# Average pooling over windows of 16: VectorE sums whole tiles, GpSimd's fold stays in the last two tiles

## The chip, the cores and the metric

The kernel runs on one core of one Trainium2 chip. The time is the device time of one execution in microseconds (us), as the median of several executions. A separate execution is recorded by the hardware profiler; its span runs from the first to the last instruction of the core.

## The reference

The input is 32 x 256 rows of 4096 float32 values, and the output has 256 values for each row. Each output is the mean of its own window of 4096 / 256 = 16 neighbouring values:

```python
for i in range(output_size):
    start = int(i * length / output_size)
    end = int((i + 1) * length / output_size)
    result[:, :, i] = np.mean(x[:, :, start:end], axis=-1)
```

134.2 MB are read and 8.4 MB are written. There is one addition for each value read, and nothing is read twice.

## The kernel before

The 8192 rows are cut into 16 tiles of 512 rows. In a tile each of the 128 partitions holds four rows, that is 1024 windows ("cells") of 16 values, 64 KB; a tile is 8.39 MB. Tiles 0 to 14 are laid out so that a partition's rows, and its outputs, are contiguous over the fifteen tiles (`x_many`, `o_many`); the last tile is laid out by itself.

There are two input buffers, `xin0` and `xin1`, used in turn, and one result tile `res` that holds the sums of all 16 tiles. SyncE issues all loads (line 63). The first two go out at once. Each later one, that of tile t + 2, is issued after SyncE has waited for the semaphore `summed` to say that tile t has been summed (line 100), because it overwrites the same buffer.

A tile is worked on as follows, with m = 512, half of the cells:

- GpSimd waits for the landing of the tile and folds the second half of the cells in place: in each window the last eight values are added to the first eight (line 81).
- VectorE waits for the same landing, sums the first half's windows of 16 (line 88), then waits for GpSimd's fold (semaphore `folded`, line 89) and sums the second half's windows, by now of eight (line 90). That instruction counts `summed` up.
- ScalarE waits for `summed` and multiplies the tile's 1024 sums by 1/16 in place (line 95), counting `scaled` up.

Each engine takes its instructions in the order in which they are written, and only the semaphores order the engines among each other. After the loop SyncE issues the store of tiles 0 to 14 when 15 tiles have been scaled (line 105), then that of the last tile (line 107). Both stand in the same DMA queue as the loads.

Of the kernel before, what the change touches and what calls it, by code (L numbers as in the profile page):

```python
# [1 line left out]

# [4 lines left out]


@with_exitstack
def kernel(  # L10
    ctx: ExitStack,
    tc: tile.TileContext,
    x: bass.AP,
    output_size: int,
    out: bass.AP,
):
    nc = tc.nc
    F32 = mybir.dt.float32
    X = mybir.AxisListType.X

    batch, channels, length = x.shape
    ob, oc, olen = out.shape
    assert ob == batch and oc == channels and olen == output_size
    assert length % output_size == 0
    window = length // output_size
    hw = window // 2
    inv_w = 1.0 / float(window)

    P = nc.NUM_PARTITIONS
    R = 4  # L30
    rows = batch * channels
    assert rows % (P * R) == 0
    ntiles = rows // (P * R)
    many = (ntiles - 1) * R
    cells = R * output_size
    m = cells // 2
    cols = R * length

    xr = x.rearrange("b c l -> (b c) l")
    orow = out.rearrange("b c o -> (b c) o")  # L40
    x_many = xr[0 : P * many, :].rearrange("(p r) l -> p (r l)", p=P, r=many)
    o_many = orow[0 : P * many, :].rearrange("(p r) o -> p (r o)", p=P, r=many)
    x_last = xr[P * many :, :].rearrange("(p r) l -> p (r l)", p=P, r=R)
    o_last = orow[P * many :, :].rearrange("(p r) o -> p (r o)", p=P, r=R)

    nbuf = 2
    xin = [
        nc.alloc_sbuf_tensor(f"xin{i}", [P, cells, window], F32, align_bytes=256)
        for i in range(nbuf)
    ]  # L50
    res = nc.alloc_sbuf_tensor("res", [P, ntiles * cells], F32, align_bytes=256)


    landed = [nc.alloc_semaphore(f"landed{i}") for i in range(nbuf)]
    folded = nc.alloc_semaphore("folded")
    summed = nc.alloc_semaphore("summed")
    scaled = nc.alloc_semaphore("scaled")
    stored = nc.alloc_semaphore("stored")

    def load(t):  # L60
        src = x_last if t == ntiles - 1 else x_many[:, t * cols : (t + 1) * cols]
        dst = xin[t % nbuf][:, :, :].rearrange("p o w -> p (o w)")
        dma = nc.sync.dma_start(out=dst, in_=src)  # L63
        dma.then_inc(landed[t % nbuf], 16)
        return dma.ins.name

    for t in range(nbuf):  # L70
        tc.info.no_tile_sem_insts.add(load(t))
    tc.close()
    tc.compile()  # L73

    for t in range(ntiles):
        xt = xin[t % nbuf]
        lo, mid, hi = t * cells, t * cells + m, (t + 1) * cells
        here = 16 * (t // nbuf + 1)

        nc.gpsimd.wait_ge(landed[t % nbuf], here)  # L80
        nc.gpsimd.tensor_add(  # L81
            out=xt[:, m:cells, 0:hw],
            in0=xt[:, m:cells, 0:hw],
            in1=xt[:, m:cells, hw:window],
        ).then_inc(folded, 1)

        nc.vector.wait_ge(landed[t % nbuf], here)
        nc.vector.reduce_sum(out=res[:, lo:mid], in_=xt[:, 0:m, :], axis=X)  # L88
        nc.vector.wait_ge(folded, t + 1)
        nc.vector.reduce_sum(  # L90
            out=res[:, mid:hi], in_=xt[:, m:cells, 0:hw], axis=X
        ).then_inc(summed, 1)

        nc.scalar.wait_ge(summed, t + 1)
        nc.scalar.mul(  # L95
            out=res[:, lo:hi], in_=res[:, lo:hi], mul=inv_w
        ).then_inc(scaled, 1)

        if t + nbuf < ntiles:
            nc.sync.wait_ge(summed, t + 1)  # L100
            load(t + nbuf)

    done = (ntiles - 1) * cells
    nc.sync.wait_ge(scaled, ntiles - 1)
    nc.sync.dma_start(out=o_many, in_=res[:, 0:done]).then_inc(stored, 16)
    nc.sync.wait_ge(scaled, ntiles)
    nc.sync.dma_start(out=o_last, in_=res[:, done:]).then_inc(stored, 16)
    for s in (*landed, folded, summed, scaled):
        nc.sync.sem_clear(s)
    nc.sync.wait_ge(stored, 32)  # L110
    nc.sync.sem_clear(stored)


# [1 line left out]
_INS = ['x', 'output_size']  # L115
_OUTS = [((32, 256, 256), 'float32')]

_NUMBERS = {'output_size': 256}


# [26 lines left out]
```

## Time and profile before

| | |
|---|---|
| median of 3 runs | 333.61 us (333.47 to 333.75) |
| the profiled execution | 333.56 us, span 332.3 us |
| bytes read, written | 134.22 MB, 8.39 MB |
| mean rate over the span | 429 GB/s |
| VectorE (DVE) busy | 209.7 us, 63% |
| GpSimd (POOL) busy | 139.7 us, 42% |
| ScalarE (ACT) busy | 18.2 us, 5% |

In the profile's rows DVE is VectorE, POOL is GpSimd, ACT is ScalarE and SPq is the sequencer of SyncE, which issues the DMAs. A group's row gives the line of the kernel, the engine, the operation, the tile written and the tiles read with their shapes (partitions x elements), the count, then busy time in all, the mean of one in ns, and the idle time of the engine ahead of them with what ended it. A row of the timeline gives the start, the duration, the instruction, and in brackets the engine's idle time ahead of it and what ended that. The landing of a load is the moment at which its semaphore has its full count.

### The profile page before, as it was taken

Reading aid. Unit: us, or ns where it says so; the run is one execution under the profiler, and the core shown is the slowest. Engines: PE = TensorE matmul, PEld = TensorE weight load, DVE = VectorE, ACT = ScalarE, POOL = GpSimd, SP = SyncE. Lnnn points to the kernel's source line nnn. Section 1 sums busy time; section 2 is a strip of 40 time slices with the busy share of each in tenths; the row PEclk is TensorE's granted clock in tenths of the full one; section 3 lists DMA queues with packets and bytes.
Section 4 is the critical chain, followed back from the end, with each engine's and each line's share of the span. In section 5 each row is a group of like instructions: output and inputs, shape, how many; then the busy total and the mean of one; then the engine's idle time right before and its main releaser. Section 6 shows DMA issues by size and latency. Waiting matters only on the chain.

```text
span 332.3 us, 130 instructions
## 1 busy us (share of the span) xinstructions
DVE 209.7 (63%) x32; ACT 18.2 (5%) x17; POOL 139.7 (42%) x20
## 2 busy tenths in 40 slices
DVE  0029396692939669292966939295693929568392
ACT  1000101001010100001010000101000010100001
POOL 0028091542709164270906437090633709063370
DMA  9898999989898999989898998989899998989997
GB/s 379 379 505 379 489 394 434 450 379 505 379 497 387 473 410 402 481 379 505 379 497 387 434 450 379 505 379 505 379 481 402 426 458 379 505 379 497 371 473 300
DMA packets 2592, 142.61 MB, mean 429 GB/s; under 512 B 288, under 2 KB 288, under 8 KB 416
## 3 DMA queue, kind: packets, MB, share of 16 engines
q1 hardware_dynamic: 2592, 142.61, 99.4%
HBM read 134.22 MB, written 8.39 MB: 429 GB/s over the span
## 4 chain that ended last, share of the span: by engine, by line
DMA 66%; POOL 21%; DVE 11%; ACT 0%; issue 0%; SPq 0%
DMA xin<-in_x_dram 66%; POOL xin L81 21%; DVE res L90 11%; ACT res L95 0%; SPq L63 0%
## 5 line engine op out<-in xcount | busy, mean ns | idle before, releaser
L81 POOL TENSOR_TENSOR xin<-xin 128x4096 f32<-128x4096 f32 x16 | 139.5, 8718 | 181.7 <-DMA xin<-in_x_dram 181.7
L88 DVE TENSOR_REDUCE res<-xin 128x512 f32<-128x8192 f32 x16 | 139.0, 8686 | 114.7 <-DMA xin<-in_x_dram 114.7
L90 DVE TENSOR_REDUCE res<-xin 128x512 f32<-128x4096 f32 x16 | 70.7, 4420 | 1.8
L95 ACT ACTIVATE res<-res 128x1024 f32<-128x1024 f32 x16 | 16.9, 1056 | 306.7 <-DVE res L90 306.7
L95 ACT ACT_TABLE_LOAD x1 | 1.3, 1283 | 2.4 <-PEq L73 2.4
L128 POOL MEMSET const-float32-0.0<- 128x1 f32 x1 | 0.1, 98 | 0.2 <-issue 0.2
L128 POOL MEMSET const-bfloat16-1.0<- 128x1 bf16 x1 | 0.1, 101 | 0.0
L128 POOL MEMSET const-uint8-127<- 128x1 uint8 x1 | 0.1, 101 | 0.0
L128 POOL MEMSET const-float32-1.0<- 128x1 f32 x1 | 0.1, 98 | 0.0
## 6 DMA issues: line engine op xcount, KB each, us to landing
out_dram<-res SPq DMA_DIRECT2D x1, 7680.0 KB, 23.4
out_dram<-res SPq DMA_DIRECT2D x1, 512.0 KB, 5.0
xin<-in_x_dram SPq DMA_DIRECT2D x16, 25.4
```

The source lines that it names most:

```text
L81: nc.gpsimd.tensor_add(out=xt[:, m:cells, 0:hw], in0=xt[:, m:cells, 0:hw], in1=xt[:, m:cells, hw:window],).then_inc(folded, 1)
L88: nc.vector.reduce_sum(out=res[:, lo:mid], in_=xt[:, 0:m, :], axis=X)
L90: nc.vector.reduce_sum(out=res[:, mid:hi], in_=xt[:, m:cells, 0:hw], axis=X).then_inc(summed, 1)
L95: nc.scalar.mul(out=res[:, lo:hi], in_=res[:, lo:hi], mul=inv_w).then_inc(scaled, 1)
L128: nc = _bacc.Bacc("TRN2", target_bir_lowering=False, num_devices=1)
```

## The change

For tiles 0 to 13 (`behind`, the number of tiles that are left, is over 2) VectorE sums all 1024 windows of 16 values in one instruction, which counts `summed` up; GpSimd has nothing to do. For tiles 14 and 15 the work stays as it was: GpSimd folds the second half, VectorE sums the first, waits for the fold, and sums the second. The count that VectorE waits for becomes 1 and 2 there. Loads, multiplies and stores are not edited.

```diff
+        behind = ntiles - t
 
         nc.vector.wait_ge(landed[t % nbuf], here)
-        nc.vector.reduce_sum(out=res[:, lo:mid], in_=xt[:, 0:m, :], axis=X)
-        nc.vector.wait_ge(folded, t + 1)
-        nc.vector.reduce_sum(
-            out=res[:, mid:hi], in_=xt[:, m:cells, 0:hw], axis=X
-        ).then_inc(summed, 1)
+        if behind <= 2:
+            nc.gpsimd.wait_ge(landed[t % nbuf], here)
+            nc.gpsimd.tensor_add(
+                out=xt[:, m:cells, 0:hw],
+                in0=xt[:, m:cells, 0:hw],
+                in1=xt[:, m:cells, hw:window],
+            ).then_inc(folded, 1)
+            nc.vector.reduce_sum(out=res[:, lo:mid], in_=xt[:, 0:m, :], axis=X)
+            nc.vector.wait_ge(folded, 3 - behind)
+            nc.vector.reduce_sum(
+                out=res[:, mid:hi], in_=xt[:, m:cells, 0:hw], axis=X
+            ).then_inc(summed, 1)
+        else:
+            nc.vector.reduce_sum(
+                out=res[:, lo:hi], in_=xt[:, :, :], axis=X
+            ).then_inc(summed, 1)
```

The fold and its wait, which stood ahead of VectorE's wait for every tile, are the lines under `if behind <= 2` now.

More of the change, by code (lines that the diff above doesn't have):

```diff
@@ L78 @@
         here = 16 * (t // nbuf + 1)
[L80 to L85, printed above, removed]
-        nc.vector.wait_ge(landed[t % nbuf], here)
-        nc.vector.reduce_sum(out=res[:, lo:mid], in_=xt[:, 0:m, :], axis=X)
-        nc.vector.wait_ge(folded, t + 1)
-        nc.vector.reduce_sum(
-            out=res[:, mid:hi], in_=xt[:, m:cells, 0:hw], axis=X
-        ).then_inc(summed, 1)
+        behind = ntiles - t
+        nc.vector.wait_ge(landed[t % nbuf], here)
+        if behind <= 2:
[14 more added lines that the diff above has]
+            ).then_inc(summed, 1)
         nc.scalar.wait_ge(summed, t + 1)
```

## The prediction

> **What bounds the kernel now.** I read the page first, then the groups by line, then the timeline around one tile, and last the DMA share in chosen stretches.
>
> ```profile
> span 332.3 us, 130 instructions
> ...
> q1 hardware_dynamic: 2592, 142.61, 99.4%
> ...
> DMA 66%; POOL 21%; DVE 11%; ACT 0%; issue 0%; SPq 0%
> ...
> L81 POOL TENSOR_TENSOR xin<-xin 128x4096 f32<-128x4096 f32 x16 | 139.5, 8718 | 181.7 <-DMA xin<-in_x_dram 181.7
> L88 DVE TENSOR_REDUCE res<-xin 128x512 f32<-128x8192 f32 x16 | 139.0, 8686 | 114.7 <-DMA xin<-in_x_dram 114.7
> L90 DVE TENSOR_REDUCE res<-xin 128x512 f32<-128x4096 f32 x16 | 70.7, 4420 | 1.8
> ```
>
> The chain that ended last gives POOL 21% and DVE 11%, as if a third of the time hung on arithmetic. The queue's line says otherwise: packets keep the 16 DMA engines busy for 99.4% of the span. Both are true, because the chain steps back through "the buffer came free" even where the freed buffer's load then stood in line behind another load. The timeline shows that line:
>
> ```profile
> 31.62 4.42 DVE L90 TENSOR_REDUCE res<-xin 128x512 f32<-128x4096 f32 x1
> 36.07 19.62 SPq L63 DMA_DIRECT2D xin<-in_x_dram  x2
> ...
> 42.11 8.69 DVE L88 TENSOR_REDUCE res<-xin 128x512 f32<-128x8192 f32 x1 [6.07 <-DMA xin<-in_x_dram]
> 42.16 8.72 POOL L81 TENSOR_TENSOR xin<-xin 128x4096 f32<-128x4096 f32 x1 [10.57 <-DMA xin<-in_x_dram]
> 50.91 4.42 DVE L90 TENSOR_REDUCE res<-xin 128x512 f32<-128x4096 f32 x1
> ...
> 61.44 8.69 DVE L88 TENSOR_REDUCE res<-xin 128x512 f32<-128x8192 f32 x1 [6.12 <-DMA xin<-in_x_dram]
> ```
>
> Tile 0 is started on at 22.82 us, tile 1 at 42.11, tile 2 at 61.44: one tile every 19.32 us. VectorE is done with tile 0 at 36.04, SyncE issues the load of tile 2 at 36.07 (0.03 later), and that load waits behind the load of tile 1 until about 41 to 42 us. So the kernel is bound by its transfers, and the compute has a **lead** of 6.07 us over them, VectorE's idle time ahead of each tile. What matters is whether a load still has a predecessor in the queue when it is issued, and that needs the time that a load takes into an empty queue. Only the first load shows it:
>
> ```profile
> L63 SPq DMA_DIRECT2D xin<-in_x_dram x16: 327/328/426, 0.7 to 287.2; - x16
> ...
> DMA to landing us min/median/max: 22.1/25.4/40.9
> ```
>
> The least time to landing, 22.1, is this one's: issued at 0.74, VectorE begins at 22.82, so 22.08 us. The DMA share by stretch takes it apart (columns: stretch, its length, busy time of DVE, ACT and POOL, clock, DMA share, GB/s; a packet counts whole in the stretch in which it starts, hence shares above 1):
>
> ```profile
> 0.00:1.75 1.75, 0.00 (x0) 0.00 (x0) 0.20 (x4) 1.00 0.00 0
> 1.75:2.12 0.37, 0.00 (x0) 0.00 (x0) 0.00 (x0) 1.00 8.04 2657
> 2.12:2.63 0.51, 0.00 (x0) 0.25 (x1) 0.00 (x0) 1.00 0.00 0
> 2.63:2.64 0.01, 0.00 (x0) 0.01 (x1) 0.00 (x0) 1.00 16.16 6554
> ...
> 12.00:20.00 8.00, 0.00 (x0) 0.00 (x0) 0.00 (x0) 1.00 1.19 516
> 21.70:22.47 0.77, 0.00 (x0) 0.00 (x0) 0.00 (x0) 1.00 3.15 1362
> 22.47:24.10 1.63, 1.28 (x1) 0.00 (x0) 1.23 (x1) 1.00 0.00 0
> 24.00:32.00 8.00, 7.89 (x2) 0.00 (x0) 7.59 (x1) 1.00 1.19 516
> ```
>
> No packet starts in the 1.0 us after the issue. Then 15 engines start a 64 KB packet each between 1.75 and 2.12 (2657 GB/s for 0.37 us is 15 x 65536 bytes), and the 16th at 2.63. The 15 take 8.04 x 0.37 x 16 / 15 = 3.17 us each, the late one 16.16 x 0.01 x 16 = 2.59. A packet with a predecessor takes 3.15 x 0.77 = 2.42 us. Each engine carries 8 of them in a load (8.39 MB over 16 engines, 64 KB each): 8 x 2.42 = 19.35, the 19.32 of the period. The second load's packets have all started by 22.47, so the first load ended there, and VectorE began 0.36 us later. An empty queue thus costs 22.08 - 19.34 = 2.74 us beyond the data: 1.0 to the first packet, up to 0.4 of spread (1.9 on the late engine), 0.75 for the slower first packet, 0.36 at the end.
>
> **The change, part by part.**
>
> *VectorE.* For tiles 0 to 13, 8.69 + 4.42 us in two instructions become one over 16384 elements, which no row shows. The two rows give the slope: (8686 - 4420) / 4096 = 1.0415 ns per element, and 4420 - 4096 x 1.0415 = 154 ns fixed. So 154 + 16384 x 1.0415 = **17.22 us**. The upper bound is twice the half tile, 17.37; the lower is 17.06, with no fixed part. I take the line through both rows. GpSimd ran beside the 8686 and not beside the 4420, and one slope with a small constant fits both, so I count nothing for GpSimd's absence. Against today's 31.62 + 4.42 - 22.82 = 13.22 us VectorE holds the tile 4.00 us longer, and the lead shrinks from 6.07 to 2.07 us. VectorE itself stays under the 19.32 of a tile and is no bound.
>
> *GpSimd.* Fourteen folds of 8.72 us and 14 waits of VectorE for them go. They lay beside VectorE's first half (8.72 against 8.69), so what they held up is inside the 13.22. That they no longer touch memory buys the transfers nothing: the share is 1.19 from 12 to 20 us, where no engine works, and 1.19 from 24 to 32, where VectorE and GpSimd both do.
>
> *ScalarE, SyncE.* The multiply (1.06 us) starts 4 us later and frees no buffer. SyncE's wait before each load moves from 13.22 to 17.22 us after the landing. Queued behind it on SyncE are only later loads and the stores, so nothing else is held. No store is moved past anything: the large one goes out after tile 14, which is still folded.
>
> *The loads.* This is the term that decides. Load t+2 goes out 17.22 + 0.03 = 17.25 us after tile t's start. If it finds the queue as the first load did, it lands 22.08 us later, less 0.10 because the first issue took 426 ns and the usual one 328: 21.98. So tile t+2 starts 17.25 + 21.98 = 39.23 us after tile t, where the transfers alone allow 2 x 19.32 = 38.64. A **stall of 0.59 us**. In other words: the packets are ready 1 to 1.9 us after the issue, the lead is 2.07, and the start of VectorE itself lags the last byte by 0.36, so the engines run dry just when the new load arrives, and its first packets come at the slower 3.17.
>
> The stall comes on every other load. Tile 2 is 0.59 late, so the load of tile 3, issued at its own time, has 0.59 more lead: tile 1's start + 39.23 equals tile 2's start + 19.32, and it just fits. Tile 4 stalls again. The loads issued after tiles 0, 2, 4, 6, 8, 10 and 12 stall: 7 x 0.59 = **4.1 us**. From tile 14 on the work is the same, and the ending (large store behind the last load, last tile's 13.2 us beside it, small store) moves as a whole.
>
> Sum: the profiled execution took 333.56 us (span 332.3 and 1.3 around it); 333.56 + 4.1 = **337.7**. The median of the runs is 333.61, 0.05 away, so the sum stands for it too.
>
> Bounds of the unknown cost, an empty queue's price in mid-kernel: nothing below (the new load is seen early enough and costs only its data, 333.6), and above the first load's whole 22.08 with a VectorE time of 17.37: 17.40 + 22.08 - 38.64 = 0.84, x 7 = 5.9, 339.5. I take the first load's row with the usual issue, the only transfer that shows the state in question.
>
> A page speaks against this. The Trainium skill, "DMA: Bandwidth & Descriptors", section "Anatomy of one DMA — SWDGE (gpsimd) path", gives a transfer as about 2.0 us plus its bytes at 436 GB/s. As an estimate that is 21.24 us for a load, 17.25 + 21.24 = 38.49, just under 38.64: no stall, 333.6. This case's first load shows 2.74 rather than 2.0, and 0.36 us after the last byte where the page puts most of the 2 us; its fit is for another issue path.
>
> **The rivals.**
>
> *Not slower: the queue never runs dry.* The stall vanishes if the price beyond the data is under 38.64 - 17.25 - 19.34 = 2.05 us. That is so if the 0.75 of the slow first packets was the first touch of a memory at rest and the late engine a start-up matter too: then 1.38 + 8 x 2.42 + 0.36 - 0.10 = 21.0, and 17.25 + 21.0 = 38.25, 0.39 to spare. Time 333.6. For it: only one cold load is on show, and it is the first of all. Against it: between loads the packet time never strays from 2.42, so a slower first packet looks like a read that nothing overlapped. The page's rule above would give the same. Chance 0.18.
>
> *Half the stall.* The slow first packet does not return but the late engine does: 1.90 + 2.59 + 7 x 2.42 + 0.36 - 0.10 = 21.69, stall 0.30, 7 x 0.30 = 2.1: 335.7. Chance 0.16.
>
> *Every load stalls.* If the time won by tile 3's load does not reach the queue (its engines' order shifts), 14 x 0.59 = 8.3: 341.9. Against it stands the arithmetic above. Chance 0.04.
>
> *The change doesn't give the long instruction I count on*, because GpSimd's reads had slowed VectorE and it is now quicker: it would have to be 0.6 us quicker than 17.22 to remove the stall, and the two rows' common slope leaves no room. Even then the transfers bound it at 333.6. Faster by some accident of the transfers: 0.02.
>
> **How the numbers follow.** Forecast 0.60 at 337.7; the others 0.18, 0.16, 0.04 and 0.02. About 0.2% (0.7 us) is what a measurement of this kernel tells from no change. Slower: 0.60 + 0.16 + 0.04 = 0.80; same 0.18; faster 0.02. The range takes in the bounds of the unknown price, 333.5 to 339.5.
>
> **What would show it.** Right: one VectorE row of about 17.22 us x14; tiles starting 19.3 and 19.9 us after one another in turn; loads issued some 21.9 us before their landing on even tiles and more on odd ones; a DMA share of some 98%. If the spacing stays at 19.3 throughout, the queue did not run dry. Wrong in another way: VectorE over 17.4, or both parities late.

## The result, and the profile after

The changed kernel takes **350.8 us** (median of 6 runs, 349.78 to 352.37) against 333.54 (333.39 to 333.75) before: the ratio is 1.0519 (95% interval 1.0505 to 1.0534). It is 17.3 us slower. I had forecast slower, but 337.7 us and at most 339.5.

These lines of the changed kernel's page answer to those of before:

```profile
span 351.1 us, 102 instructions
...
q1 hardware_dynamic: 2592, 142.61, 96.5%
...
DMA 60%; DVE 36%; POOL 2%; ACT 0%; issue 0%; SPq 0%
...
L95 DVE TENSOR_REDUCE res<-xin 128x1024 f32<-128x16384 f32 x14 | 241.1, 17220 | 65.6 <-DMA xin<-in_x_dram 65.6
...
L84 POOL TENSOR_TENSOR xin<-xin 128x4096 f32<-128x4096 f32 x2 | 17.4, 8720 | 322.5 <-DMA xin<-in_x_dram 322.5
L89 DVE TENSOR_REDUCE res<-xin 128x512 f32<-128x8192 f32 x2 | 17.4, 8687 | 11.7 <-DMA xin<-in_x_dram 11.7
```

VectorE's long sum takes 17220 ns, the 17.22 of the prediction, and VectorE still waits for loads and for nothing else. The same packets now fill 96.5% of a longer span. VectorE's rows in the timeline of the changed kernel show where the time goes:

```profile
22.79 17.22 DVE L95 TENSOR_REDUCE res<-xin 128x1024 f32<-128x16384 f32 x1 [22.79 <-DMA xin<-in_x_dram]
42.06 17.22 DVE L95 TENSOR_REDUCE res<-xin 128x1024 f32<-128x16384 f32 x1 [2.06 <-DMA xin<-in_x_dram]
63.69 17.22 DVE L95 TENSOR_REDUCE res<-xin 128x1024 f32<-128x16384 f32 x1 [4.41 <-DMA xin<-in_x_dram]
83.28 17.22 DVE L95 TENSOR_REDUCE res<-xin 128x1024 f32<-128x16384 f32 x1 [2.37 <-DMA xin<-in_x_dram]
105.63 17.22 DVE L95 TENSOR_REDUCE res<-xin 128x1024 f32<-128x16384 f32 x1 [5.13 <-DMA xin<-in_x_dram]
125.46 17.22 DVE L95 TENSOR_REDUCE res<-xin 128x1024 f32<-128x16384 f32 x1 [2.62 <-DMA xin<-in_x_dram]
144.79 17.22 DVE L95 TENSOR_REDUCE res<-xin 128x1024 f32<-128x16384 f32 x1 [2.11 <-DMA xin<-in_x_dram]
167.51 17.22 DVE L95 TENSOR_REDUCE res<-xin 128x1024 f32<-128x16384 f32 x1 [5.50 <-DMA xin<-in_x_dram]
...
331.65 8.69 DVE L89 TENSOR_REDUCE res<-xin 128x512 f32<-128x8192 f32 x1 [9.33 <-DMA xin<-in_x_dram]
```

Tiles 1 to 4 start 19.27, 21.63, 19.59 and 22.35 us after the tile ahead of each. So far the pattern is the forecast one, a late tile and one at about the old pace, but the late ones lose 2.3 and 3.0 us where I had 0.59. Then it breaks: tile 6 comes at the old pace (19.33), and the late ones after it are tiles 7, 11, 13 and 15 (22.72, 22.33, 22.01 and 22.55). Six late tiles lose 17.7 us against a pace of 19.32, and tile 15 starts at 331.65 instead of 312.91, 18.7 later. Before the change no spacing ahead of the last tile was above 19.38.

The first late load is issued at 40.04. The DMA share by stretch of the changed kernel shows when its packets start (columns as in the prediction; packets of the load ahead of it that still move have started earlier, so they don't count):

```profile
39.40:41.40 2.00, 0.61 (x1) 1.06 (x1) 0.00 (x0) 1.00 0.00 0
41.40:41.85 0.45, 0.00 (x0) 0.00 (x0) 0.00 (x0) 1.00 4.60 1602
41.85:42.50 0.65, 0.44 (x1) 0.00 (x0) 0.00 (x0) 1.00 0.58 202
42.50:43.14 0.64, 0.64 (x1) 0.00 (x0) 0.00 (x0) 1.00 0.92 307
43.14:43.70 0.56, 0.56 (x1) 0.00 (x0) 0.00 (x0) 1.00 0.00 0
```

Rate times length over 64 KB gives 11, 2 and 3 packets: eleven engines start 1.4 to 1.8 us after the issue, the last one at 43.13, 3.1 us after it. The load ahead of it ended on its engines between 41.06 and 41.74, so that engine stood dry for about 1.4 us or more, and the tile lands when the last engine is done.

### The profile page after: what moved, and what is told of

The parts are those of the page before. It is cut to its first block, busy times and chain, and to the rows that moved or that the text cites. A ratio compares the mean times of both kernels' runs of the same rounds, so it can differ in the third digit from the quotient of the medians.

```text
span 351.1 us, 102 instructions
## 1 busy us (share of the span) xinstructions
DVE 267.3 (76%) x18; ACT 18.2 (5%) x17; POOL 17.6 (5%) x6
## 3 DMA queue, kind: packets, MB, share of 16 engines
q1 hardware_dynamic: 2592, 142.61, 96.5%
## 4 chain that ended last, share of the span: by engine, by line
DMA 60%; DVE 36%; POOL 2%; ACT 0%; issue 0%; SPq 0%
DMA xin<-in_x_dram 60%; DVE res L95 34%; POOL xin L84 2%; DVE res L91 1%; ACT res L100 0%; SPq L63 0%
## 5 line engine op out<-in xcount | busy, mean ns | idle before, releaser
L95 DVE TENSOR_REDUCE res<-xin 128x1024 f32<-128x16384 f32 x14 | 241.1, 17220 | 65.6 <-DMA xin<-in_x_dram 65.6
L84 POOL TENSOR_TENSOR xin<-xin 128x4096 f32<-128x4096 f32 x2 | 17.4, 8720 | 322.5 <-DMA xin<-in_x_dram 322.5
L89 DVE TENSOR_REDUCE res<-xin 128x512 f32<-128x8192 f32 x2 | 17.4, 8687 | 11.7 <-DMA xin<-in_x_dram 11.7
L91 DVE TENSOR_REDUCE res<-xin 128x512 f32<-128x4096 f32 x2 | 8.8, 4420 | 0.2
```

The costliest lines, as they stand in the source:

```text
L84: nc.gpsimd.tensor_add(out=xt[:, m:cells, 0:hw], in0=xt[:, m:cells, 0:hw], in1=xt[:, m:cells, hw:window],).then_inc(folded, 1)
L91: nc.vector.reduce_sum(out=res[:, mid:hi], in_=xt[:, m:cells, 0:hw], axis=X).then_inc(summed, 1)
L95: nc.vector.reduce_sum(out=res[:, lo:hi], in_=xt[:, :, :], axis=X).then_inc(summed, 1)
```

## The experiments

Theory A: a load that is issued while another one is moving gets its first packets late, and engines that have run dry by then lose that time. Its rivals are named in each expectation. Every median of the kernel before in these comparisons is between 333.39 and 333.59.

**How much lead is needed.** In tiles 0 to 13 of the kernel before, VectorE's full share of the 1024 cells is moved (512 before, all in the changed kernel):

```diff
-    m = cells // 2
+    half = cells // 2
...
+        m = 768 if ntiles - t > 2 else half
         lo, mid, hi = t * cells, t * cells + m, (t + 1) * cells
```

640 cells: 

> In tiles 0 to 13 VectorE sums 640 of the 1024 cells in full and GpSimd folds 384; VectorE holds a tile about 14.2 us (before 13.2, changed 17.2), so a load is issued some 5.1 us ahead of the next tile's start. Theory A, late packets: a load that is issued while another one moves gets its first packets 1.4 to 3.8 us after the issue (the changed kernel's rows), and what it gets later than an engine has run dry is lost; here the engines finish 4.1 to 4.8 us after the issue, so nothing is lost: 333.5. Theory B, the empty queue's price of my prediction (1.0 to 1.9 us to the first packet, 0.75 for a slow one): 333.5. Theory C, the transfers suffer from VectorE's longer sums or from GpSimd's absence, not from the lead: a quarter of the fold is gone, so about a quarter of the loss of 17.3 us, 337.8.

768 cells: 

> As m640 with 768 cells in full and 256 folded: VectorE holds a tile about 15.2 us, lead 4.1 us, engines finish 3.0 to 3.7 us after the issue. Theory A: only the latest packets (3.1 to 3.8 us) come too late, 333.5 to 336. Theory B: 333.5. Theory C: half of the loss, 342.2.

832 cells: 

> As m768 with 832 cells in full and 192 folded: VectorE holds a tile about 15.8 us, lead 3.5 us, engines finish 2.5 to 3.2 us after the issue. Theory A, late packets: between m768 (333.9 at 4.1 us of lead) and m896 (343.9 at 3.0), as the latest packets come 3 to 3.8 us after the issue: 335 to 340. Theory B, a threshold at 2.7 us of lead: 333.5.

896 cells: 

> As m640 with 896 cells in full and 128 folded: VectorE holds a tile about 16.3 us, lead 3.0 us, engines finish 1.9 to 2.6 us after the issue. Theory A: the late engines run dry on many loads, 338 to 345. Theory B: 16.3 + 21.98 = 38.3 stays under 38.64, so 333.5. Theory C: three quarters of the loss, 346.5.

Measured, with VectorE's shortest idle time ahead of a tile as the lead:

| cells in full | lead, us | median, us | ratio to before (95%) |
|---|---|---|---|
| 512 (before) | 6.06 | 333.5 | |
| 640 | 5.21 | 333.47 | 0.9998 (0.9988 to 1.0007) |
| 768 | 4.15 | 333.91 | 1.0013 (1.0002 to 1.0024) |
| 832 | 3.61 | 341.28 | 1.0234 (1.0189 to 1.028) |
| 896 | 3.08 | 343.92 | 1.031 (1.028 to 1.034) |
| 1024 (changed) | 2.06 | 350.8 | 1.0519 (1.0505 to 1.0534) |

Theory C (the loss follows GpSimd's missing share) falls: with half of the fold gone nothing measurable over 0.4 us is lost. Theory B, my prediction's price, falls too: it had no loss down to 2.7 us of lead, and there are 7.8 us at 3.61. The loss sets in between 4.15 and 3.61 us, where theory A's 3 to 3.8 us to the last packet put it; at 832 cells it came out 1.3 us above A's own range.

A late start is not the whole of it. In the kernel with 832 cells tile 2 is on time and tile 3 is the first late one, 20.45 us after tile 2. These are the stretches in which the first 16 packets of the two loads start:

```profile
41.00:41.80 0.80, 0.00 (x0) 0.00 (x0) 0.00 (x0) 1.00 3.03 1311
60.35:61.10 0.75, 0.00 (x0) 0.00 (x0) 0.00 (x0) 1.00 3.69 1398
```

Both loads start on all engines within 0.8 us, as the load ahead of them ends. But the first packets of the second one take 2.77 us on average (3.69 x 0.75) against 2.42, and the slowest of them 3.4.

**The lead alone, with all of the old work.** The kernel before with one more sum on VectorE, whose end lets the load go:

```diff
-        nc.vector.reduce_sum(
+        last = nc.vector.reduce_sum(
             out=res[:, mid:hi], in_=xt[:, m:cells, 0:hw], axis=X
-        ).then_inc(summed, 1)
+        )
+        if ntiles - t > 2:
+            if t > 0:
+                nc.vector.wait_ge(summed, t)
+            last = nc.vector.reduce_sum(
+                out=junk[:, :], in_=xt[:, m : m + 458, 0:hw], axis=X
+            )
+        last.then_inc(summed, 1)
```

> The kernel before with all of GpSimd's folds, and in tiles 0 to 13 a third VectorE instruction of about 4.0 us (458 windows of 8 summed into a tile that nobody reads) that alone lets the next load go. The lead is that of the changed kernel, 2.1 us, the work that of the kernel before and a little more. Theories A and B, the lead alone counts: the changed kernel's time, 350.8 within 2. Theory C, the long sum or GpSimd's absence is what hurts: 333.5.

It took 346.96 us (median of 4 runs: three from 345.19 to 347.36 and one of 352.18; ratio 1.0382). No fold was taken away, and most of the loss is there: theory C falls again. It is 3.8 us under the changed kernel, outside the 2 us that theories A and B allowed. Its lead is a little longer (2.19 against 2.06 us); between 896 and 1024 cells 6.9 us are lost over 1.02 us of lead, so that explains about 0.9. For the rest there was a direct trial.

**GpSimd put back beside the long sum:**

```diff
-            nc.vector.wait_ge(folded, 3 - behind)
+            nc.vector.wait_ge(folded, t + 1)
...
         else:
+            nc.gpsimd.wait_ge(landed[t % nbuf], here)
+            if t > 0:
+                nc.gpsimd.wait_ge(folded, t)
+            nc.gpsimd.tensor_add(
+                out=junk[:, :, :],
+                in0=xt[:, m : m + 480, 0:hw],
+                in1=xt[:, m : m + 480, hw:window],
+            ).then_inc(folded, 1)
             nc.vector.reduce_sum(
...
+            nc.sync.wait_ge(folded, t + 1)
             nc.sync.wait_ge(summed, t + 1)
```

> The changed kernel, with GpSimd adding 480 cells' halves of every tile 0 to 13 into a scratch tile that nobody reads, beside VectorE's long sum. The load waits for both, VectorE ends last, so lead and VectorE's work are the changed kernel's and GpSimd works as before the change. It tells whether the 3.8 us between delay (347.0) and the changed kernel (350.8) come from GpSimd's absence. Theory A, the lead alone counts: 350.8 within 1.5. Theory C in a weak form, GpSimd's absence costs part of it: 347.

It took 350.61 us (ratio 1.0531, 1.0503 to 1.0558), the changed kernel's time. These are its groups:

```profile
L104 DVE TENSOR_REDUCE res<-xin 128x1024 f32<-128x16384 f32 x14 | 241.1, 17220 | 64.9 <-DMA xin<-in_x_dram 64.9
L99 POOL TENSOR_TENSOR junk<-xin 128x3840 f32<-128x3840 f32 x14 | 114.6, 8186 | 182.0 <-DMA xin<-in_x_dram 182.0
```

GpSimd works 8.19 us beside every long sum, which keeps its 17220 ns, and the loss stays: GpSimd's absence is no part of it. The other 3 us by which the delayed kernel was quicker stay unexplained: three of its four runs lie below the changed kernel's quickest, 349.78.

**Every other load.** VectorE sums whole tiles only where t is even:

```diff
+        fold = behind <= 2 or t % 2 == 1
...
-        if behind <= 2:
+        if fold:
...
-            nc.vector.wait_ge(folded, 3 - behind)
+            nc.vector.wait_ge(folded, (t + 1) // 2 if behind > 2 else t - 6)
```

> VectorE sums whole tiles only for the even ones among 0 to 13; odd tiles are folded by GpSimd as before. Seven loads (of tiles 2, 4 to 14) are issued with the short lead of 2.1 us, the others with 6.1. My prediction counted on this pattern by itself: in the changed kernel every other load stalls, and the one between has the time won. Theory G, that still holds, only each stall is 2.3 us and more: 333.5 + 7 x 2.3 to 2.5 = 350 to 351, the changed kernel's time. Theory H, the loss of each short lead is its own: half of 17.3, 342.

It took 348.19 us (ratio 1.0443, 1.0411 to 1.0474): seven short leads cost 14.7 us, 2.1 each on average, 85% of the changed kernel's loss. VectorE's rows:

```profile
22.64 17.22 DVE L96 TENSOR_REDUCE res<-xin 128x1024 f32<-128x16384 f32 x1 [22.64 <-DMA xin<-in_x_dram]
41.93 8.69 DVE L90 TENSOR_REDUCE res<-xin 128x512 f32<-128x8192 f32 x1 [2.07 <-DMA xin<-in_x_dram]
...
63.87 17.22 DVE L96 TENSOR_REDUCE res<-xin 128x1024 f32<-128x16384 f32 x1 [8.72 <-DMA xin<-in_x_dram]
83.27 8.69 DVE L90 TENSOR_REDUCE res<-xin 128x512 f32<-128x8192 f32 x1 [2.17 <-DMA xin<-in_x_dram]
```

Tile 2 comes 21.94 us after tile 1, tile 3 again 19.40 after tile 2. Of the seven tiles with a short lead, five lose 1.9 to 2.7 us in this trace, tiles 8 and 14 only 0.4 and 0.6. Theory G stands (a little under its 350), theory H (342) does not: stalls on half of the loads are enough for most of the loss. That the changed kernel stalls strictly on every other load is not shown; its late tiles are 2, 4, 7, 11, 13 and 15.

**VectorE does all the work, with the lead kept.** Half loads into half buffers, each loaded again as soon as it is summed; in the second kernel (R = 2, four buffers) tiles of half the size:

```diff
+        for h in range(2):
+            nc.vector.wait_ge(landed[2 * (t % nbuf) + h], here)
+            nc.vector.reduce_sum(
+                out=res[:, lo + h * m : mid + h * m],
+                in_=xt[:, h * m : (h + 1) * m, :],
+                axis=X,
+            ).then_inc(summed, 1)
...
+            for h in range(2):
+                nc.sync.wait_ge(summed, 2 * t + h + 1)
+                load(t + nbuf, h)
```

> GpSimd has no work at all; VectorE sums every tile in two halves of 8.69 us, each half is loaded by its own DMA (32 KB per partition) and its buffer half is loaded again as soon as it is summed. VectorE's time per tile is 17.4 us, as long as in the changed kernel, but the queue always holds at least one and a half halves when a load is issued (lead over 10 us). Theories A and B: 333.5 within 1. Theory C, VectorE's long sums or GpSimd's absence hurt the transfers: about 350.

> GpSimd has no work; tiles of half the size in four buffers (the same bytes of buffer), VectorE sums each in one instruction of 8.69 us. A load is issued when three more stand in the queue or move, lead some 20 us. Theories A and B: 333.5 within 1. Theory C: about 350.

Half loads: 333.68 us (ratio 1.0006, 0.9996 to 1.0015), with VectorE busy for 277.9 us and GpSimd unused. The whole loss is gone, so VectorE's work by itself cost no time, only the lead that it took. Small tiles: 335.06 (ratio 1.0053, 1.0037 to 1.007), 0.6 over the expectation's range. The timeline of that kernel's end shows the likely place:

```profile
312.65 0.35 SPq L95 DMA_DIRECT2D out_dram<-res  x1
312.95 8.69 DVE L80 TENSOR_REDUCE res<-xin 128x512 f32<-128x8192 f32 x1 [0.99 <-DMA xin<-in_x_dram]
```

The large store is issued 0.3 us before VectorE starts on the last tile, as the last load is just done, where the kernel before issues it 5.3 us ahead (307.61 against 312.91). That store finds a dry queue. I read this off the rows and did not try it by itself.

**What an empty queue costs.** The kernel before with one load at a time (the first one alone ahead of the loop):

```diff
-        if t + nbuf < ntiles:
-            nc.sync.wait_ge(summed, t + 1)
-            load(t + nbuf)
+        if t + 1 < ntiles:
+            nc.sync.wait_ge(landed[t % nbuf], here)
+            if t > 0:
+                nc.sync.wait_ge(summed, t)
+            load(t + 1)
```

> The kernel before with one load in flight at a time: load t+1 is issued when load t has landed, so every load finds an empty queue and nothing else moves. It gives sixteen samples of the price of an empty queue where the first load gave one. Theory A, packets come late because another load is moving at the issue: each load lands about 22.0 us after its issue as the first did, tiles start 22.0 us after one another, 333.5 + 15 x (22.0 - 19.32) = 374. Theory D, any load in mid-kernel is dearer than the first one (23.6 to 24.8 us as in the changed kernel): 333.5 + 15 x (4.3 to 5.5) = 398 to 416. Theory E, the first load is dear because it is the first: 21.3, 363.

371.96 us. The loads' landing times, and the packets of the second load, which is issued at 22.56:

```profile
DMA to landing us min/median/max: 21.6/21.8/23.2
```

```profile
22.56:23.50 0.94, 0.94 (x1) 0.00 (x0) 0.89 (x1) 1.00 0.00 0
23.50:23.95 0.45, 0.45 (x1) 0.00 (x0) 0.45 (x1) 1.00 6.07 2039
23.95:24.15 0.20, 0.20 (x1) 0.00 (x0) 0.20 (x1) 1.00 1.86 655
```

Fourteen packets start 0.94 to 1.39 us after the issue and the other two by 1.6. Over all loads the last engine starts after 1.7 us on average, and a first packet takes 3.09 us against 2.42. So the first load's 22.08 was a fair sample of an empty queue (theory A), not a special case of the start (E) nor cheaper than mid-kernel (D). What I had wrong is that the changed kernel's queue is not empty at the issue.

**A second queue for every other load:**

```diff
-        dma = nc.sync.dma_start(out=dst, in_=src)
+        eng = nc.scalar if t % 2 == 0 and t > 0 else nc.sync
+        dma = eng.dma_start(out=dst, in_=src)
...
         nc.scalar.wait_ge(summed, t + 1)
+        if t % 2 == 0 and t + nbuf < ntiles:
+            load(t + nbuf)
...
-        if t + nbuf < ntiles:
+        if t % 2 == 1 and t + nbuf < ntiles:
```

First with the odd tiles on ScalarE: 

> The changed kernel with the loads of odd tiles issued by ScalarE, so that they go through a queue of their own; tile t+2's load no longer stands behind tile t+1's in one queue. Theory F, a new load's packets come late because they stand in order behind the other load's in the same queue: the loss mostly goes, 333.5 to 340. Theory A as it stands, any moving transfer delays them: 348 to 354.

Then as in the diff: 

> As twoq, but the first two loads both go out from SyncE, one behind the other, so that tiles still land one after another; from then on the loads of even tiles are issued by ScalarE and those of odd ones by SyncE. twoq could not tell, since its first two loads ran beside each other and landed together. Theory F, a new load's packets come late because they stand in order behind the other load's in the same queue: the loss mostly goes, 333.5 to 340. Theory A as it stands, any moving transfer delays them: 348 to 354.

371.46 and 352.80 us. The first told nothing, since its first two loads shared the engines from the start and landed together at 41.89. In the second, the first load that ScalarE issues is a clean sample, the only one: issued at 39.91 behind nothing in its own queue, its packets start between 41.35 and 42.83, 1.4 to 2.9 us after the issue, as late as before. From the next load on, the two queues again share the engines and tiles land in pairs. As far as that one load tells, order within one queue (F) is not the reason.

**Smaller packets.** Each load as four DMAs of 16 KB per partition:

```diff
+        q = cols // 4
+        for k in range(4):
+            dma = nc.sync.dma_start(
+                out=dst[:, k * q : (k + 1) * q], in_=src[:, k * q : (k + 1) * q]
+            )
+            dma.then_inc(landed[t % nbuf], 16)
...
-        here = 16 * (t // nbuf + 1)
+        here = 64 * (t // nbuf + 1)
```

> The changed kernel with every load issued as four DMAs of 16 KB per partition, back to back at the same moment, so that a packet has 16 KB instead of 64. Lead, bytes and VectorE's work stay the same. Theory P, a new load's first packet comes late because it waits for whole packets in progress (2.4 us each): packets of 0.6 us make the delay and the spread of the engines smaller, 336 to 343. Theory A with a delay that does not depend on packets: 349 to 353.

350.45 us (ratio 1.0501, 1.0464 to 1.0539): the size of the packets (P) is not the reason either.

**What must be moving.** As the kernel with one load at a time, but the load goes out when its tile has been summed, and a small transfer 4.5 us ahead of it:

```diff
+            nc.sync.wait_ge(folded, t + 1)
+            if t > 0:
+                nc.sync.wait_ge(copied, 16 * t)
+            nc.sync.dma_start(out=junk[:, :], in_=x_last[:, 0:3840]).then_inc(copied, 16)
+            nc.sync.wait_ge(summed, t + 1)
+            load(t + 1)
```

A read: 

> As serial (one load at a time), but each next load is issued when its tile has been summed, 13.3 us after landing, and 4.5 us before it a small read goes out, of 15 KB per partition from the input into a scratch tile that nobody uses; its packets end about 2 us after the load's issue. So a load is issued while a read is moving, with some 2 us to the dry queue as in the changed kernel. Theory A, a moving transfer delays a new load's first packets: 23 to 24.8 us from issue to start of the tile, 36.3 to 38 us per tile, 587 to 614 in all. Theory without a delay: 21.8 us as in serial, 35.1 per tile, 569.

A copy: 

> As readbusy, but the small transfer copies 15 KB per partition from the tile's own buffer to the scratch tile, so that the DMA engines are busy while nothing is read from the chip's main memory. Theory R, reads in flight make a new load's first packets late: no delay here, 21.8 us per load, 569. Theory E, busy DMA engines or queues make them late whatever they move: as readbusy, 587 to 614.

A shorter copy: 

> As copybusy with 11.5 KB per partition instead of 15: in copybusy the copy's packets (0.80 us each) ended 3.6 us after the load's issue, too late to compare with readbusy; here they should end 1.9 to 2.1 us after it, as readbusy's do. Theory E, busy DMA engines delay a new load whatever they move: the last engine starts 2.6 us or more after the issue, 36.3 us per tile and more, 587 to 600. Theory R, only reads from main memory do: the last start within 2.1 us, 35.1 us per tile, 569.

A store: 

> As readbusy, but the small transfer writes 15 KB per partition from the tile's buffer into the output, which the real stores write again at the end. Theory R, reads in flight: 569. Theory E, any transfer: 587 to 614.

A longer store: 

> As storebusy with 24 KB per partition instead of 15: in storebusy the stores' packets had ended 1.1 us after the load's issue, when an empty queue would just give the first packets, so it told little (22.0 us per load, serial 21.8). Here they should end some 3.7 us after it. The load then waits its turn until 3.7; what counts is how long after that the last engine starts. Theory E: 0.5 to 1.0 us after the end of the stores, as in readbusy and copybusy, 24.5 us per load or more, 608 or more. Theory R: all engines start as the stores end, 23.5 us, 593.

Medians were 590.17, 620.61, 575.90, 576.13 and 610.98 us. From the packets of the 15 loads (means; starts and ends in us after the load's issue; the path is the median spacing of the tiles, less the 13.25 us from a tile's start to the next issue where something is in flight):

| in flight | its packets end | last engine starts | a first packet takes | path of the load |
|---|---|---|---|---|
| nothing (one load at a time) | - | 1.70 | 3.09 | 21.8 |
| read, 15 KB | 2.10 | 2.61 | 2.94 | 23.2 |
| copy, 11.5 KB | 2.17 | 2.24 | 2.58 | 22.1 |
| copy, 15 KB | 3.57 | 4.28 | 2.56 | 25.1 |
| store, 15 KB | 1.10 | 1.73 | 3.22 | 22.2 |
| store, 24 KB | 4.79 | 4.80 | 2.53 | 24.5 |

With a read in flight the load takes 23.2 us, as theory A expected; the shorter copy, whose packets end as late, leaves it at 22.1. In the stretches after the load's issue, first of the kernel with the read (issued at 35.81), then of that with the shorter copy (36.06), the difference is in the last packets:

```profile
35.81:37.30 1.49, 0.00 (x0) 1.06 (x1) 0.00 (x0) 1.00 0.94 402
37.30:37.93 0.63, 0.00 (x0) 0.00 (x0) 0.00 (x0) 1.00 2.99 1089
37.93:38.60 0.67, 0.00 (x0) 0.00 (x0) 0.00 (x0) 1.00 1.66 587
```

```profile
36.06:37.70 1.64, 0.00 (x0) 1.06 (x1) 0.00 (x0) 1.00 1.00 266
37.70:38.26 0.56, 0.00 (x0) 0.00 (x0) 0.00 (x0) 1.00 3.88 1521
38.26:38.60 0.34, 0.00 (x0) 0.00 (x0) 0.00 (x0) 1.00 1.37 578
```

Both small transfers end 2.1 to 2.2 us after the issue. Beside the copy all engines have started 2.33 us after the issue (at 38.39); beside the read six start from 2.1 us on, the last after 2.8. The shorter copy and the longer store speak for theory R (reads in flight delay a load, other traffic only makes it queue). The longer store took the time that theory E named (611 us, 608 or more), but only because its packets ended at 4.79 us where 3.7 had been expected; the load started as they ended. The longer copy speaks against theory R: its last engine starts 0.7 us after the copy's end, and its 620.61 us lie outside both expectations. So I hold as shown that loads issued beside moving reads come late on average, but not each: in the changed kernel tiles 6, 9 and 10 start 21.9, 21.8 and 21.8 us after their loads' issue, about as long as with nothing in flight. What decides it, and why one copy does it too, stays open.

## Why the prediction was wrong

**Right:** that the kernel is bound by its transfers and lives on their lead; VectorE's 17.22 us and the lead of 2.07 (2.06 measured); that GpSimd's absence moves nothing (GpSimd put back: 350.6); that the loss comes from late and slow first packets of loads with a short lead; that a stalled load leaves time to the next one, so that only about half of the loads pay (seven short leads alone: 14.7 of 17.3 us), though not strictly in turn; that the ending moves as a whole.

**Wrong:** the size of one term, the path of a load with a short lead. The failing step is "I take the first load's row with the usual issue, the only transfer that shows the state in question." It shows another state. The first load, and each of the loads that went out one at a time (21.8 us), is issued with nothing moving. The changed kernel issues the first of its late loads 1.0 to 1.7 us before the engines run dry, with reads in flight, and the path there is 23.2 us in the isolated trial and 23.65 (63.69 - 40.04) for that load. By the prediction's own sum 17.25 + 23.2 - 38.64 = 1.8 us a stall, times 7 is 12.7: near the 14.7 of seven short leads. In the changed kernel's trace the late loads are dearer still: those of tiles 2, 4, 7, 11, 13 and 15 take 23.65, 24.69, 24.80, 24.42, 24.05 and 24.90 us from issue to start, 24.42 on average where the prediction had 21.98. With that the sum gives 17.25 + 24.42 - 38.64 = 3.0 us a stall, times 6 is 18.2, of the 18.7 us by which tile 15 is later in that run. So the term that was mis-sized is the path, and the stalls are fewer and far larger than forecast. The trace also shows that engines that start late finish late, and that the load behind them starts with the same spread; how much of the extra path over 23.2 us this makes I did not measure.

Two judgements followed from that step. The upper bound, 339.5, held only for an empty queue and was no bound: I had excluded that a queue about to run dry could be dearer than an empty one. And the first rival, no loss at all, had 0.18 because I looked for reasons why mid-kernel should be cheaper than the start, not dearer.

The 2.0 us plus bytes of the Trainium skill ("DMA: Bandwidth & Descriptors", section "Anatomy of one DMA — SWDGE (gpsimd) path"), which spoke for no stall, is off here by more than my own figure: 21.8 us against the estimate of 21.24 with an empty queue, 23.2 with reads in flight. The Trainium skill, "DMA: Bandwidth & Descriptors", section "Latency and other measured facts", has the access to main memory at 0.2 us on average and 2 us at high load. That would fit the dearer start beside reads, but no run here measures one access, and by itself it does not give the late engines beside the 15 KB copy.

The changed kernel's DMA share, forecast at some 98%, is 96.5%, which is the same error seen from the other side.

No kernel here beats the one before: 333.47 (640 cells) and 333.68 (half loads, without GpSimd) are the same within their intervals.

## What to carry to other kernels

In a kernel bound by its transfers, an engine off the path still owns the lead: compute how long before the queue runs dry the next load is issued, and treat a change that eats the lead as a change on the path. Here 4.2 us of lead were enough and 3.6 were not, and half-buffer loads gave the lead back without the second engine. A transfer's price measured with nothing in flight is no upper bound for one that is issued while others are ending.

## What the runs showed of the hardware

- A load issued beside moving reads started on its last engine 2.6 us after the issue on average (3.1 for the first one in the changed kernel) against 1.7 with nothing in flight, and its path was 23.2 us against 21.8. The 23.2 hold the 2.1 us until the read's own packets have ended; beside a copy that ends as late the path was 22.1. Single loads vary: among those with a short lead in the changed kernel some took 21.8 us.
- A first packet of 64 KB took 3.09 us on average when nothing else moved and 2.42 behind another load in the kernel before; in the kernel with 832 cells those of one load took 2.77 us on engines that show no gap ahead of them.
- Two loads in two queues share the engines and land together: with the loads of odd tiles on ScalarE's queue the first two tiles both started on loads that were done at 41.89, and the kernel took 371.46 us.
- A copy within the core's buffers was slower per packet than a read of the same size: 0.79 us against 0.57 for 15 KB (medians).
